# Input projections of the even block: TensorE's instructions tied to the order in which they are written

## The chip, the cores and the metric

One core of one Trainium2 chip runs the whole program. The metric is the device time of one execution in microseconds (us), as the median of several runs.

## The reference, cut to what matters

The model is a chain of blocks on 1024 tokens of width 1024. The change touches the first one, the even block, and in it only the products of the normed tokens `h` and the normed context `hc` with the input weights. The filters of the next block (`hyena_filters` and their Fourier transforms) and the modulation vectors of blocks 0 and 1 do not depend on `h`; the kernel computes them beside these products.

```python
shift, scale, gate = modulation(c[:, None, :], w_mod[i], b_mod[i])
h = rmsnorm(x, norm_g[i]) * (1 + scale) + shift
hc = rmsnorm(ctx, norm_g[i]) * (1 + cscale) + cshift
a_val, a_gate, q, k, v, b_gate = jnp.split(h @ w_in, EVEN_SPLITS, axis=-1)
q = apply_rope(rmsnorm(to_heads(q, N_Q_HEADS), q_norm_g[li]), cos, sin)
k = apply_rope(rmsnorm(to_heads(k, N_KV_HEADS), k_norm_g[li]), cos, sin)
ck, cv = jnp.split(hc @ w_in[:, EVEN_SPLITS[2]:EVEN_SPLITS[4]], 2, axis=-1)
...
def modulation(cond, w_mod, b_mod):
    m = jax.nn.silu(cond) @ w_mod + b_mod
```

## The kernel before, in words

**The products.** Every float32 product of an activation and a weight is made of three matmuls on rounded halves (`mm3`, L200 to L204): high by high, low by high, high by low. `gemm` (L206) does that for the eight slices of the inner dimension, 24 matmuls of 512 columns for one half of the tokens. `ev_in` (L440) makes 18 panels of 128 output columns for all 1024 tokens with it, 48 matmuls a panel: six gates (PSUM tile `pbg`), two pool values and two pool gates (`pav`, `pag`), six queries (`pq`) and two keys (`pk`, with the context's keys `pck` ahead of each), and then the values (`pv`). The first two gates are done together, half by half (`pg2`), so that their first 96 matmuls can start on the half of the tokens that is normed first. A panel's PSUM tile has two buffers, small PSUM tiles share four buffers (`psb`).

**The side work.** After each slice of a `gemm`, that is after every three matmuls (six for the values), `self.go()` (L124) advances three generators, each at its own rate:

- `K.hy`, rate 0.7: `hy_prep` (L856), which makes the filters' spectra in 12 units (`hy_spectrum`, L888). A unit has four tap products `pf` (L902, L903), column sums `pl` (L924) of the sum `hacc` that VectorE and ScalarE make of the taps, a turned row (L935), and two blocks of Fourier products `pk` (L953, L954), which VectorE then combines (`dft8`, L811). Between these steps stand bare `yield`s, among them five ahead of `pl`. The step before the first unit (`load(0)`, L864) loads the table `w`, splits it into `w3h` and `w3l` on ScalarE and VectorE, and copies each from partitions 0 to 63 to partitions 64 to 127 by a DMA from the POOL queue (L870). The taps read all 128 partitions.
- `K.ctx`, rate 0.2: the context's norm (`ctx_norm`, L367).
- `K.side`, rate 0.1: `modulation1` (L964), four times `mod_cols` (L309): eight steps, each with a DMA of 512 KB (`wm`, L315) and a multiply-add on VectorE into `macc` (L318, L320), and with the eighth step, at once, eight one-column matmuls that sum `macc` over partitions (`pm`, L220) and an addition on VectorE (L325).

```python
    def go(self):                       # class Work
        self.due += self.rate
        while self.due >= 1.0:
            self.due -= 1.0
            next(self.gen, None)
```

So the written order is fixed by counting: the n-th call of `go` runs a step of `K.hy` whenever 0.7 n passes a whole number, one of `K.side` at every tenth call. The second call runs `load(0)`, the third the first taps; the eighth steps of `mod_cols` fall on calls 80, 160, 240 and 320 of 344.

**The order on the engines.** The written order is not the order in which an engine gets its instructions. When the program is built, each engine's list is laid out anew: among the instructions whose inputs and buffers are expected to be ready by then, the one written first. On the chip each engine then takes its list in that order. What a DMA queue, VectorE, ScalarE and TensorE get is settled in this way for the whole program.

**Buffers.** Tiles of 4 KB a partition (the tables, `wm`, `hk`, `fS`, queries and so on) share 40 slots (`t`, L153). The tile of a load is given out where the load is written, and its DMA waits until the slot's last reader is done.

Of the kernel before, what the change touches and what calls it, by code (L numbers as in the profile page):

```python
# [44 lines left out]
class Work:  # L45


    def __init__(self, gen, rate=0.0):
        self.gen, self.rate, self.due = gen, rate, 0.0

    def go(self):
# [4 lines that stand above are left out]
# [48 lines left out]
class Core:  # L104
    def __init__(self, tc, ctx, d):
        self.tc, self.nc, self.d = tc, tc.nc, d
        nc = self.nc
        self.pool = ctx.enter_context(tc.tile_pool(name="sb", bufs=1))
        self.psum = ctx.enter_context(tc.tile_pool(name="ps", bufs=1, space=PSUM))
        self.dram = ctx.enter_context(tc.tile_pool(name="dr", bufs=1, space=DRAM))  # L110
        self.ident = self.c("ident", [P, P])
        make_identity(nc, self.ident)
        self.inv = self.c("inv", [P, 4])
        nc.gpsimd.memset(self.inv[:, 0:1], 1.0 / D)
        nc.gpsimd.memset(self.inv[:, 1:2], 1.0 / P)
        nc.gpsimd.memset(self.inv[:, 2:3], 1.0)
        nc.gpsimd.memset(self.inv[:, 3:4], 0.0)
        self.mhalf = self.c("mhalf", [P, 8])
        nc.gpsimd.memset(self.mhalf, -0.5)
        self.vec = self.c("vec", [P, NVEC])  # L120
        nc.sync.dma_start(self.vec, d["vecs"])
        self.work = []

    def go(self):  # L124
        for w in self.work:
            w.go()

    def steps(self, n):
        for _ in range(n):
            self.go()  # L130
# [2068 lines left out]
def build(tc, d, out):  # L2199
    with ExitStack() as ctx:  # L2200
        K = Core(tc, ctx, d)
        K.hy = Work(K.hy_prep(), 0.7)
        hs, hc = K.ev_norm()
        K.load_consts()
        K.ctx = Work(K.ctx_norm(hc), 0.2)
        K.side = Work(K.modulation1(), 0.1)
        K.work = [K.hy, K.ctx, K.side]
        ks, vs, scls = K.ev_in(hs, hc)
        K.hy.drain()
        K.side.drain()  # L2210
        K.side = Work(K.s5_prep(), 0.25)
        K.work = [K.side]
        y = K.ev_attn(ks, vs, scls)
        x1_d = K.scr("x1_d", [KT, P, L])
        K.side.rate = 0.14
        hs = K.ev_out(y, x1_d)
        K.side.rate = 0.02
        y = K.od_mix(hs)
        K.side.rate = 0.1
        K.od_out(y, x1_d)  # L2220
        K.work = []
        K.block2(out)
# [14 lines left out]
```

## Time and profile before

| | us |
|---|---|
| median of 3 runs (4068.89 to 4072.51) | 4070.12 |
| the profiled execution | 4067.31 |
| its span | 4065.5 |
| TensorE busy in the span | 3800.5 |
| mean granted TensorE clock, share of full | 0.967 |

The span runs from the first to the last instruction of the program. The page gives busy time by engine, forty slices of the span, the DMA queues, the chain that ended last, and the costliest groups of instructions. The input projections lie between 57 and 534 us of the span: the first `pbg` matmul starts at 57.4, the last `pv` matmul ends at 534.1. The stage is read below by windows, by the waits of TensorE, and by the timeline. A busy window's clock is the share of full speed that was granted: 1.00 is 2.4 GHz, 0.50 is 1.2 GHz.

### The profile page before, as it was taken

Reading aid. Unit: us, or ns where it says so; the run is one execution under the profiler, and the core shown is the slowest. Engines: PE = TensorE matmul, PEld = TensorE weight load, DVE = VectorE, ACT = ScalarE, POOL = GpSimd, SP = SyncE. Lnnn points to the kernel's source line nnn. Section 1 sums busy time; section 2 is a strip of 40 time slices with the busy share of each in tenths; the row PEclk is TensorE's granted clock in tenths of the full one; section 3 lists DMA queues with packets and bytes.
Section 4 is the critical chain, followed back from the end, with each engine's and each line's share of the span. In section 5 each row is a group of like instructions: output and inputs, shape, how many; then the busy total and the mean of one; then the engine's idle time right before and its main releaser. Section 6 shows DMA issues by size and latency. Waiting matters only on the chain.

```text
span 4065.5 us, 51267 instructions
## 1 busy us (share of the span) xinstructions
PE 3800.5 (93%) x19684; PEld 3145.8 (77%) x19684; DVE 2841.9 (70%) x4892; ACT 1445.5 (36%) x2328; POOL 308.7 (8%) x533
## 2 busy tenths in 40 slices
PE   7899899899999997799999999989999899999998
PEld 4778788778788866687788888878787677888886
DVE  5676767786888778667866664458878867666545
ACT  3222245533111221433423333335555634332332
POOL 0001100041010022000000000011010000000000
PEclk8999999999999998999999999989999899999999
DMA  6433321063222248513322245323232332122443
GB/s 235 138 113 128 111 77 42 28 212 130 73 73 74 98 148 253 164 53 103 125 80 76 94 153 171 122 83 99 73 99 73 89 124 109 73 94 78 170 159 111
DMA packets 172907, 458.35 MB, mean 113 GB/s; under 512 B 38542, under 2 KB 59028, under 8 KB 172662
## 3 DMA queue, kind: packets, MB, share of 16 engines
q1 hardware_dynamic: 129254, 317.94, 23.8%
q0 software_dynamic: 41104, 132.41, 9.9%
q10 hardware_dynamic: 2304, 4.72, 0.3%
q8 instruction: 155, 2.54, 0.3%
q14 instruction: 90, 0.74, 0.1%
HBM read 327.07 MB, written 100.66 MB: 105 GB/s over the span
## 4 chain that ended last, share of the span: by engine, by line
PE 75%; DVE 13%; issue 4%; DMA 3%; ACT 3%; POOL 1%; SPq 0%; POOLq 0%; DVEq 0%; ACTq 0%
PE p L202 7%; PE p L203 7%; PE p L204 7%; PE pd L202 4%; PE pd L204 4%; PE pd L203 4%; PE pout L202 2%; PE pout L204 2%; PE pout L203 2%; DVE sbm L1964 2%; PE pu L202 2%; PE pu L204 2%; PE pu L203 2%; PE pwt L1985 1%; PE pz L1047 1%
## 5 line engine op out<-in xcount | busy, mean ns | idle before, releaser
L185 DVE TENSOR_TENSOR wl<-wt,wh 128x1024 fp32r<-128x1024 f32 x232 | 283.3, 1222 | 276.5 <-ACT wh L184 274.1
L184 ACT CAST wh<-wt 128x1024 fp32r<-128x1024 f32 x232 | 242.9, 1048 | 653.5 <-PE pd L203 189.9
L202 PE MATMUL p<-tq,wq 128*128 128x512 f32 x736 | 290.5, 395 | 3.6 <-ACT wq L215 3.6
L203 PE MATMUL p<-tq,wq 128*128 128x512 f32 x736 | 290.0, 394 | 0.0
L204 PE MATMUL p<-tq,wq 128*128 128x512 f32 x736 | 290.0, 394 | 0.0
L202 PE MATMUL pd<-hd,wh 128*128 128x512 f32 x704 | 277.7, 394 | 2.8 <-DVE r L1831 2.8
L204 PE MATMUL pd<-hd,wl 128*128 128x512 f32 x704 | 276.5, 393 | 0.0
L203 PE MATMUL pd<-hd,wh 128*128 128x512 f32 x704 | 276.3, 393 | 0.0
L203 PE MATMUL p<-hq,wq 128*128 128x512 f32 x480 | 189.7, 395 | 0.0
L202 PE MATMUL p<-hq,wq 128*128 128x512 f32 x480 | 189.4, 395 | 0.0
L204 PE MATMUL p<-hq,wq 128*128 128x512 f32 x480 | 189.0, 394 | 0.0
L215 ACT CAST wq<-ws 128x512 fp32r<-128x512 f32 x184 | 114.3, 622 | 208.7 <-PE p L204 204.0
L1723 DVE TENSOR_TENSOR fsg<-fsg,p 128x512 f32<-128x512 f32 x140 | 94.4, 686 | 117.1 <-PE p L204 117.1
L202 PEld LDWEIGHTS p<-tq,wq 128*128 128x128 f32 x736 | 138.1, 188 | 43.3 <-ACT wq L215 4.9
L204 PEld LDWEIGHTS p<-tq,wq 128*128 128x128 f32 x736 | 138.3, 188 | 32.2
L203 PEld LDWEIGHTS p<-tq,wq 128*128 128x128 f32 x736 | 138.2, 188 | 30.6
L1723 DVE TENSOR_TENSOR fsu<-fsu,p 128x512 f32<-128x512 f32 x140 | 94.5, 687 | 93.7 <-PE p L204 93.6
L216 DVE TENSOR_TENSOR wq<-ws,wq 128x512 fp32r<-128x512 f32 x184 | 126.7, 690 | 46.4 <-ACT wq L215 44.5
L202 PEld LDWEIGHTS pd<-hd,wh 128*128 128x128 f32 x704 | 132.2, 188 | 33.9 <-DVE r L1831 4.2
L204 PEld LDWEIGHTS pd<-hd,wl 128*128 128x128 f32 x704 | 132.2, 188 | 31.2 <-DVE wl L185 0.6
L203 PEld LDWEIGHTS pd<-hd,wh 128*128 128x128 f32 x704 | 132.2, 188 | 30.0
L202 PE MATMUL pu<-hq,wh 128*128 128x512 f32 x320 | 129.8, 406 | 9.5 <-DVE cv L984 9.5
(702 smaller groups left out, 10657.4 us busy)
## 6 DMA issues: line engine op xcount, KB each, us to landing
wt<-w_gu SPq DMA_DIRECT2D x88, 512.0 KB
wt<-w_dn SPq DMA_DIRECT2D x88, 512.0 KB
wm<-w_mod SPq DMA_DIRECT2D x48, 512.0 KB
hid<-fsg POOLq DMA_DIRECT2D x44, 512.0 KB, 3.9
hr<-hid SPq DMA_DIRECT2D x44, 512.0 KB
wt<-w_od SPq DMA_DIRECT2D x28, 512.0 KB
khat<-fX POOLq DMA_DIRECT2D x24, 512.0 KB, 3.0
kh<-khat SPq DMA_DIRECT2D x24, 512.0 KB
```

The lines of the kernel that those rows point to most:

```text
L184: nc.scalar.copy(wh, wt)
L185: nc.vector.tensor_tensor(wl, wt, wh.bitcast(F32), op=ALU.subtract)
L202: mm(ps, lh, rh, start=first, stop=False)
L203: mm(ps, lh, rl, start=False, stop=False)
L204: mm(ps, ll, rh, start=False, stop=last)
L215: self.nc.scalar.copy(h, src)
L216: self.nc.vector.tensor_tensor(l, src, h.bitcast(F32), op=ALU.subtract)
L1047: mm(p4[:, i, q], tb[:, m], z[:, self.POS[m]], start=True, stop=False)
L1723: add = lambda o, u, v: tt(o, u, v, op=ALU.add)
L1964: nc.vector.tensor_tensor_scan(om[:, :n - 1], om[:, :n - 1], self.inv[:, 3:4].to_broadcast([P, n - 1]), 1.0, op0=ALU.mult, op1=ALU.add)
L1985: nc.tensor.transpose(pt[:, s * P:(s + 1) * P], W[x][:, c:c + P], self.ident)
```

## The change

A helper `in_order` calls a function, goes through the instructions that were written meanwhile, and ties each one of TensorE to the TensorE instruction written before it. The tie is of order alone: no semaphore is added by it. `build` wraps the call of `ev_in` in it, so all 1932 TensorE instructions that are written there, the products' and the side work's, stand on TensorE in the order in which they are written. No instruction is added or removed, and VectorE's, ScalarE's, POOL's and SP's are not tied.

```diff
         self.work = []
+        self.last = None
...
+    def in_order(self, fg):
+
+        bb = self.nc.cur_bb.bb
+        n = len(bb.instructions)
+        out = fg()
+        for i in list(bb.instructions)[n:]:
+            if i.engine == mybir.EngineType.PE:
+                if self.last:
+                    self.tc.add_manual_dep(i, self.last.name, mybir.DependencyInfo(
+                        mybir.DependencyClass.NoSync, mybir.DependencyReason.DATA), reason="in_order")
+                self.last = i
+        return out
...
-        ks, vs, scls = K.ev_in(hs, hc)
+        ks, vs, scls = K.in_order(lambda: K.ev_in(hs, hc))
```

## Rows read from the trace of the kernel before

**Rows 1.** The page: busy time by engine, and the chain that ended last

```profile
PE 3800.5 (93%) x19684; PEld 3145.8 (77%) x19684; DVE 2841.9 (70%) x4892; ACT 1445.5 (36%) x2328; POOL 308.7 (8%) x533
...
PE 75%; DVE 13%; issue 4%; DMA 3%; ACT 3%; POOL 1%; SPq 0%; POOLq 0%; DVEq 0%; ACTq 0%
```

**Rows 2.** Windows over the input projections: stretch, length, busy us by engine, PEclk, DMA

```profile
57.00:534.10 477.10, 437.98 (x2532) 370.52 (x2532) 320.00 (x601) 119.11 (x171) 47.58 (x62) 0.93 0.38 127
...
57.00:106.40 49.40, 42.02 (x213) 35.42 (x213) 35.72 (x59) 19.97 (x31) 2.55 (x3) 0.85 0.52 175
106.40:133.30 26.90, 24.05 (x138) 20.36 (x137) 18.31 (x39) 5.87 (x10) 2.88 (x5) 0.94 0.32 123
133.30:166.90 33.60, 31.26 (x177) 26.55 (x176) 21.18 (x44) 7.23 (x12) 1.65 (x3) 0.95 0.35 110
166.90:209.40 42.50, 36.06 (x189) 30.50 (x188) 23.35 (x46) 10.17 (x15) 3.20 (x6) 0.88 0.48 155
...
239.80:271.30 31.50, 31.50 (x179) 26.42 (x179) 21.70 (x42) 6.75 (x11) 1.60 (x3) 1.00 0.30 101
271.30:308.50 37.20, 31.48 (x155) 24.98 (x154) 25.12 (x50) 7.25 (x9) 1.60 (x3) 0.86 0.35 128
...
343.50:364.30 20.80, 20.80 (x121) 16.54 (x120) 12.27 (x21) 3.17 (x4) 2.80 (x3) 0.84 0.39 116
...
400.30:442.80 42.50, 39.22 (x238) 33.80 (x237) 27.73 (x52) 10.72 (x15) 4.98 (x7) 0.96 0.40 138
442.80:472.80 30.00, 25.50 (x150) 21.68 (x149) 21.58 (x41) 7.53 (x11) 3.86 (x5) 0.89 0.40 138
472.80:534.10 61.30, 56.86 (x437) 51.65 (x436) 42.31 (x81) 12.22 (x19) 7.95 (x8) 0.94 0.25 87
```

**Rows 3.** Waits of TensorE from 57 to 535 us: line, releaser, us, times, longest

```profile
PE pl L924 <- DVE hacc L918: 16.6, 6, 4.7
```

**Rows 4.** Windows, the products `pbg` alone: stretch, length, TensorE busy us (count)

```profile
57.00:82.70 25.70, 24.68 (x96) 18.91 (x96) 0.00 (x0) 0.92 0.50 170
```

**Rows 5.** Tile `w3h`, 50 to 110 us: its copy's start, and its DMA's time to landing

```profile
L870 POOL DMA_DIRECT2D w3h<-w3h x1: 579/579/579, 79.7 to 79.7; - x1
...
DMA to landing us min/median/max: 2.9/2.9/2.9
```

**Rows 6.** Timeline of TensorE: start, us, instruction, idle time before it and releaser

```profile
84.27 0.36 PE L903 MATMUL pf<-w3l,hs 128*128 128x256 f32 x1 [0.86 <-DMA w3l<-w3l]
...
90.63 1.20 PE L924 MATMUL pl<-inv,hacc 128*128 128x1 f32 x5 [4.72 <-DVE hacc L918]
...
166.54 0.39 PE L954 MATMUL pk<-hk,fsin 128*128 128x128 f32 x2
...
167.22 0.40 PE L204 MATMUL pbg<-hh,wl 128*128 128x512 f32 x1
167.46 0.39 PE L202 MATMUL pbg<-hh,wh 128*128 128x512 f32 x1
...
270.26 0.39 PE L954 MATMUL pk<-hk,fsin 128*128 128x128 f32 x2
...
399.95 0.39 PE L954 MATMUL pk<-hk,fsin 128*128 128x128 f32 x2
```

**Rows 7.** Timeline of VectorE: the eighth multiply-add of three modulation vectors

```profile
174.19 1.28 DVE L320 SCALAR_TENSOR_TENSOR macc<-wm,silu_c,macc 128x1024 f32<-128x1024 f32 x1
...
278.05 1.29 DVE L320 SCALAR_TENSOR_TENSOR macc<-wm,silu_c,macc 128x1024 f32<-128x1024 f32 x1
...
406.95 1.28 DVE L320 SCALAR_TENSOR_TENSOR macc<-wm,silu_c,macc 128x1024 f32<-128x1024 f32 x1
```

**Rows 8.** Windows around two waits: length, busy by engine, PEclk

```profile
90.60:99.00 8.40, 7.25 (x33) 6.73 (x34) 3.79 (x10) 1.03 (x3) 0.00 (x0) 0.51 0.56 226
...
118.00:122.60 4.60, 4.23 (x16) 3.59 (x17) 2.35 (x8) 0.00 (x0) 0.00 (x0) 0.64 0.00 0
```

**Rows 9.** Waits of the SP queue from 57 to 535 us

```profile
SPq L315 <- PE pk L954: 50.5, 6, 12.7
```

## The prediction, made before the changed kernel was run

> **What bounds the kernel now.** I read the page first: TensorE is busy for 93% of the span and makes 75% of the chain that ended last [rows 1], so a microsecond that TensorE loses in a stage reaches the end, and one that it saves does too, as long as the next engine is not late. Then the windows over the input projections. From 57.0 to 534.1 us TensorE is busy for 437.98 of 477.10 us [rows 2]: 39.1 us idle. Its clock is 0.93 of full on the mean, so at most another 0.07 of 477, 33 us, lies in slow clock (the two overlap, since the clock is also low while it waits). VectorE, the next engine, has 320.0 us of work there, so no other engine bounds the stage. The stretches differ: 239.8 to 271.3 us has no idle time and a clock of 1.00, while 166.9 to 209.4 loses 6.4 us idle at 0.88 and 271.3 to 308.5 loses 5.7 at 0.86 [rows 2]. Last the waits: 16.6 us of the idle time are column sums `pl` waiting for `hacc`, six times, 4.7 us at the longest [rows 3].
>
> What the change can act on is order alone. By the code's count the written order has the first taps `pf` behind nine `pbg` matmuls; the trace has all 96 `pbg` matmuls of the first two gates ahead of them, done by 82.7 us [rows 4]. So the order does change where a piece of side work was expected late: there the products were pulled ahead of it. Where the side work was in time, as in 133.3 to 166.9 and 239.8 to 271.3, the trace already follows the written order (taps, 30 product matmuls, `pl`, 9, row, `pk`), and nothing moves.
>
> **The change part by part.** The work is the same; terms are waits and slow clock, in us, plus is slower. A product matmul takes 0.24 at full clock, 167.22 to 167.46 [rows 6] (0.232 over longer runs; I use 0.232).
>
> *The first taps.* They read `w3h` and `w3l` in all partitions. `w3h`'s copy is issued at 79.7 and takes 2.9 to land [rows 5], 82.6; `w3l` lets the taps go on at 84.27 [rows 6]. What leads to these copies (the table's load, the cast behind the norm's on ScalarE, the POOL queue) hangs on no product, so I leave it where it is. Tied, TensorE has nine matmuls, is through by about 61, and stands until 84.3; 87 product matmuls wait behind the taps: 87 x 0.232 = +20.2. After so long a stand it restarts at half clock: +4.1, as in 90.6 to 99.0, 8.4 us at 0.51 [rows 8]. Against that, the 87 matmuls now cover what unit 0 of the filters leaves idle today: 4.7 ahead of `pl` and, of the 7.4 idle from 57.0 to 106.4 (49.40 less 42.02 [rows 2]), another 1.8 beside the 0.9 that stays [rows 6], and the slow 4.1 that follows: -10.6. Together +13.7. Bounds: +9.6 without the slow restart, +24.3 if nothing is covered. I take the sum, since each item is a row.
>
> *Unit 1.* Today its four taps come at once, behind unit 0, and `pl` waits 2.85 (106.4 to 133.3: 26.90 less 24.05 [rows 2]), then runs 4.6 us at 0.64, 1.7 lost [rows 8]. Written, the taps lie among products: -4.5.
>
> *The modulation sums `pm`.* This is the wait that the tie adds. The eighth `wm` load is written right ahead of its multiply-add and its sum, and its slot is often given free only by `pk`: SP waits 50.5 us in six such waits [rows 9]. Written, the first sum stands 9 product matmuls behind `pk`, the second 6, the third directly behind it. Last `pk` ends: 166.93, 270.65, 400.34, start and duration added [rows 6]. `macc` ends: 175.47, 279.34, 408.23 [rows 7]. So TensorE would wait 6.4 (175.47 less 166.93 + 9 x 0.232), 7.3 (279.34 less 270.65 + 6 x 0.232) and 7.9: 21.6, and restart slowly each time, 2.9 (the mean of 4.1 and 1.7): 8.7 more. Behind each wait are queued the products of the panel, and VectorE's addition and whatever follows it there. Today that time is filled with products pulled ahead, which are then missing. So the first two stretches give back what they lose now, at most 6.4 + 0.12 x 42.5 = 11.5 and 5.7 + 0.14 x 37.2 = 10.9 [rows 2]: net 6.4+2.9-11.5 = -2.2 and 7.3+2.9-10.9 = -0.7. Around the third nothing is lost today: +10.8. Bounds for the three: -22.4 if `macc` is in time everywhere, +30.3 if nothing is given back. The fourth sum is in the right place already. I take the waits as the rows stand, since what VectorE does between `pk` and `macc` is the transform of the same unit, which follows `pk` in both kernels.
>
> Here the Trainium skill has a rule that speaks against the change: TensorE: Matmul & The Clock Gate, section on HAM oscillation, says that an engine made to wait for a DMA between pieces of its inner loop comes back at the half rate each time, and advises to finish the inner loop ahead of the wait, which is what the pulled-ahead products do. Rows 8 agree for waits of 4.7 and 2.85 us. By the rule the four new waits cost the 4.1 + 8.7 = 12.8 of slow restarts that stand in my sum; without them the sum below would be -2.7, no change.
>
> *Later waits.* 343.5 to 364.3 has no idle time but a clock of 0.84: 3.3 [rows 2]; a written order that spaces the queries' small matmuls may give back -3, bounds -3.3 and +3. From 400.3 to 534.1 the keys and values lose 3.3+4.5+4.4 = 12.2 idle and 1.7+3.3+3.7 = 8.7 in clock [rows 2]. Some waits there are for PSUM buffers that VectorE frees late, which order doesn't cure: I take -8, bounds -20.9 and +5.
>
> *New waits of `pl`.* Written, `pl` has 30 product matmuls, 7.0, behind the last tap. The need ranges from 4.7 (unit 0: 85.9 to 90.63) to some 12 (unit 1, with unit 0's transform in VectorE's way). So each of 12 units waits between nothing and 4.9; the clean stretches say mostly nothing. I take +4 in all, bounds 0 and 59.
>
> No instruction is added, VectorE's, SP's and POOL's lists are laid out by the same rule, and the attention behind the stage starts when the values end: no other term.
>
> **Sum:** 13.7 - 4.5 - 2.2 - 0.7 + 10.8 - 3 - 8 + 4 = +10.1. On the profiled execution's 4067.3 (span 4065.5 and 1.8 around it) that is 4077.4; its median of runs stands 2.8 higher, so 4070.1 + 10 = 4080. What a measurement of this kernel can tell from no change is 0.2%, 8.1 us.
>
> **The rivals.** *The sums are in time, and it is faster.* Place: the three `pm`. If VectorE's list, laid out anew, has the eighth multiply-add ahead of the transform, `macc` is done before TensorE comes to the sum. It decides when `macc` ends within 2 us of the last `pk`. For it: the first sum's load is issued long before 166. Against it: the second and third loads wait for a slot of that very `pk` [rows 9]. Price: 30.3 less, 4080 - 30 = 4050. *It cancels.* If half of the `pm` waits go, or the keys give back 17 instead of 8, the sum is between -5 and +5: 4070. Also here: the order hardly changes because it is already the written one in most units; but the 96 matmuls ahead of the first taps speak against that. *VectorE's queue is late everywhere.* If `pl` waits half of its 59 bound, because taps, ropes and pool windows meet on VectorE, +26: 4106.
>
> **How the numbers follow.** The forecast, slower by 8 to 25, has 0.37; late everywhere 0.08; it cancels 0.30; faster 0.25. So slower 0.45, same 0.30, faster 0.25. The likeliest case gives 4080; its own range is 4078 to 4095. The range for 8 in 10 reaches to the middle of the faster case, 4050, and to 4106.
>
> **What would show it.** In the changed kernel's profile the stage's first idle time should be one of some 21 us, from about 61 to 82.6, released by the copies of `w3h` and `w3l`; the wait of 4.7 ahead of the first `pl` should be gone; three waits of `pm` for `macc`, 5 to 8 us each; and the last `pv` should end near 544 instead of 534.1. I am wrong if the copies land earlier than 79, if `pm` doesn't wait, or if `pl`'s waits exceed today's 16.6 us.

## The result, and the profile of the changed kernel

The changed kernel takes 4102.27 us (median of 4 runs, 4099.78 to 4104.96), the kernel before 4071.32: 1.0079 times as long, 95% interval 1.0065 to 1.0094. It is slower, by 31 us; 10 were forecast. The two profiled executions differ by 36.6 (4103.89 less 4067.31). Their spans, 4102.1 and 4065.5, differ by as much, and 35.0 of it arise in the stage: the last `pv` matmul ends at 569.1 instead of 534.1. In the changed kernel the lines stand 14 lower (L202 is now L216).

The page first: busy times are nearly what they were [rows 1].

```profile
PE 3806.2 (93%) x19684; PEld 3153.9 (77%) x19684; DVE 2842.9 (69%) x4892; ACT 1446.2 (35%) x2328; POOL 308.9 (8%) x533
...
PE 76%; DVE 13%; issue 4%; ACT 3%; DMA 3%; POOL 1%; SPq 0%; DVEq 0%; ACTq 0%; POOLq 0%
```

Windows over the stage (stretch, length, busy us of PE, PEld, DVE, ACT, POOL, PEclk, DMA share, GB/s), which answer to [rows 2]:

```profile
57.00:569.10 512.10, 442.28 (x2530) 374.83 (x2531) 321.15 (x600) 118.82 (x170) 47.08 (x62) 0.90 0.35 118
57.00:118.00 61.00, 39.20 (x191) 31.83 (x192) 35.55 (x63) 18.20 (x29) 2.78 (x4) 0.72 0.34 114
118.00:145.80 27.80, 25.26 (x156) 21.58 (x155) 18.05 (x34) 6.94 (x11) 2.66 (x5) 1.00 0.48 171
...
175.60:218.90 43.30, 36.00 (x189) 30.18 (x188) 23.62 (x46) 10.52 (x15) 3.20 (x6) 0.84 0.48 152
249.90:281.40 31.50, 31.50 (x179) 26.40 (x178) 21.68 (x42) 6.75 (x11) 1.60 (x3) 1.00 0.29 101
281.40:326.90 45.50, 36.94 (x190) 30.70 (x189) 26.88 (x52) 7.94 (x10) 1.60 (x3) 0.85 0.30 105
326.90:361.00 34.10, 26.37 (x128) 21.88 (x127) 21.45 (x38) 11.23 (x13) 7.05 (x7) 0.84 0.49 162
361.00:400.00 39.00, 35.25 (x187) 27.71 (x186) 27.50 (x48) 8.28 (x11) 6.66 (x8) 0.96 0.33 120
400.00:440.00 40.00, 30.43 (x156) 25.70 (x157) 19.71 (x39) 5.22 (x7) 3.86 (x5) 0.79 0.29 107
```

The first row says what kind of loss it is. TensorE is idle for 512.10 less 442.28 = 69.8 us, where it was idle for 39.1: 30.7 of the 35.0 are waiting. Only 4.3 (442.28 less 437.98) are slower running. The clean stretch stays clean: 249.9 to 281.4 is the 239.8 to 271.3 of before, 31.50 busy of 31.50 at clock 1.00, only 10 us later.

The waits of TensorE from 57 to 580 us (line, releaser, us, times, longest) say for what, beside [rows 3]:

```profile
PE pm L234 <- DVE macc L334: 20.2, 3, 8.4
PE pf L916 <- DMA w3h<-w3h: 13.8, 1, 13.8
PE pl L938 <- DVE hacc L932: 12.8, 3, 7.7
...
PE pr L247 <- POOL rs_r L242: 4.3, 1, 4.3
...
PE pf L917 <- DMA w3l<-w3l: 3.3, 1, 3.3
```

And the timeline of TensorE where each of them ends, beside [rows 6], then VectorE's last multiply-adds ahead of the three sums, beside [rows 7]:

```profile
82.11 0.55 PE L916 MATMUL pf<-w3h,hs 128*128 128x256 f32 x1 [13.77 <-DMA w3h<-w3h]
85.92 0.55 PE L917 MATMUL pf<-w3l,hs 128*128 128x256 f32 x1 [3.26 <-DMA w3l<-w3l]
...
100.41 0.84 PE L938 MATMUL pl<-inv,hacc 128*128 128x1 f32 x7
...
184.21 3.57 PE L234 MATMUL pm<-inv,macc 128*128 128x1 f32 x16 [4.38 <-DVE macc L334]
...
289.57 0.77 PE L234 MATMUL pm<-inv,macc 128*128 128x1 f32 x3 [7.45 <-DVE macc L334]
...
355.58 1.83 PE L938 MATMUL pl<-inv,hacc 128*128 128x1 f32 x8 [7.72 <-DVE hacc L932]
...
401.20 1.00 PE L938 MATMUL pl<-inv,hacc 128*128 128x1 f32 x5 [3.94 <-DVE hacc L932]
...
429.14 1.01 PE L234 MATMUL pm<-inv,macc 128*128 128x1 f32 x4 [8.37 <-DVE macc L334]
```

```profile
182.87 1.28 DVE L334 SCALAR_TENSOR_TENSOR macc<-wm,silu_c,macc 128x1024 f32<-128x1024 f32 x1
...
288.13 1.28 DVE L334 SCALAR_TENSOR_TENSOR macc<-wm,silu_c,macc 128x1024 f32<-128x1024 f32 x1
...
427.81 1.28 DVE L334 SCALAR_TENSOR_TENSOR macc<-wm,silu_c,macc 128x1024 f32<-128x1024 f32 x1
```

Most of this is as foretold: the stand ahead of the first taps, the 4.72 ahead of the first `pl` gone, three waits of `pm`. Two long waits were not expected: `pl` at 355.58 and at 401.20, both while the queries are projected.

**Where the lag grows.** Matmul ends alone don't show this, since the kernel before pulls products ahead. So TensorE's matmuls of the stage are added up in the order of each trace, each at its full-clock pitch (0.232 a product, and so on), and the ends are compared at equal work. This is an estimate from one profiled execution of each kernel, good to some 1.5 us. Positive is later than the kernel before; e2 to e10 are experiments below. The third sum is written in the sixth query; the row at 390.4 is read just ahead of its wait.

| kernel before at | what has just passed | changed | e2 | e5 | e6 | e9 | e10 |
|---|---|---|---|---|---|---|---|
| 154.2 | first two gates, filter units 0 and 1 | +8.9 | +8.1 | +1.1 | +0.6 | +9.9 | +0.3 |
| 193.8 | first sum | +10.5 | +3.0 | -4.0 | -7.2 | +11.7 | -4.9 |
| 256.8 | most of the pools | +10.5 | +5.7 | -4.0 | -7.4 | +10.9 | -4.6 |
| 325.8 | second sum, first query | +14.8 | +5.9 | -0.5 | -9.7 | +10.9 | -6.6 |
| 390.4 | most of the queries, units 7 and 8 | +29.7 | +20.1 | +12.8 | -11.7 | +11.2 | -8.8 |
| 420.4 | third sum | +44.7 | +25.6 | +16.7 | -11.6 | +30.4 | -8.8 |
| 524.4 | keys and values | +35.3 | +11.7 | +1.5 | -13.3 | +20.6 | -9.5 |

So the changed kernel loses 9 at the start, 6 around the first two sums, 15 in the queries, 15 at the third sum, and gets 9 back in the keys and values.

### The profile page after: what moved, and what is told of

The parts are those of the page before. It is cut to its first block, busy times and chain, and to the rows that moved or that the text cites. A ratio compares the mean times of both kernels' runs of the same rounds, so it can differ in the third digit from the quotient of the medians.

```text
span 4102.1 us, 51264 instructions
## 1 busy us (share of the span) xinstructions
PE 3806.2 (93%) x19684; PEld 3153.9 (77%) x19684; DVE 2842.9 (69%) x4892; ACT 1446.2 (35%) x2328; POOL 308.9 (8%) x533
## 3 DMA queue, kind: packets, MB, share of 16 engines
q10 hardware_dynamic: 2304, 4.72, 0.3%
## 4 chain that ended last, share of the span: by engine, by line
PE 76%; DVE 13%; issue 4%; ACT 3%; DMA 3%; POOL 1%; SPq 0%; DVEq 0%; ACTq 0%; POOLq 0%
PE p L216 7%; PE p L218 7%; PE p L217 7%; PE pd L216 4%; PE pd L218 4%; PE pd L217 4%; PE pout L216 2%; PE pout L218 2%; PE pout L217 2%; PE pu L216 2%; PE pu L217 2%; PE pu L218 2%; DVE sbm L1978 2%; PE pwt L1999 1%; PE pz L1061 1%
## 5 line engine op out<-in xcount | busy, mean ns | idle before, releaser
L216 PE MATMUL p<-tq,wq 128*128 128x512 f32 x736 | 291.5, 396 | 3.6 <-ACT wq L229 3.6
L216 PE MATMUL pd<-hd,wh 128*128 128x512 f32 x704 | 277.6, 394 | 2.8 <-DVE r L1845 2.8
L216 PE MATMUL p<-hq,wq 128*128 128x512 f32 x480 | 189.2, 394 | 0.0
L216 PEld LDWEIGHTS p<-tq,wq 128*128 128x128 f32 x736 | 138.4, 188 | 42.4 <-ACT wq L229 4.9
L216 PEld LDWEIGHTS pd<-hd,wh 128*128 128x128 f32 x704 | 132.2, 188 | 34.0 <-DVE r L1845 4.3
L216 PE MATMUL pu<-hq,wh 128*128 128x512 f32 x320 | 129.7, 405 | 9.5 <-DVE cv L998 9.5
```

Source lines behind the costliest of these rows:

```text
L216: mm(ps, lh, rh, start=first, stop=False)
```

## The experiments

Theory A was that the loss comes from places where a piece of side work is late and its matmul now holds up products that were pulled ahead before: the first taps, three sums, and column sums of two units. Its rival was that a fixed order costs something in general, so that freeing one place moves the loss to the next. Times are medians; the first four shared a kernel before of 4071.12, the next four 4070.51, the last three 4069.51. Edits are to the changed kernel except in e6.

**e1: the sums left out of the tie.** `loose` collects the `pm` matmuls, and `in_order` passes over them.

```diff
-            if i.engine == mybir.EngineType.PE:
+            if i.engine == mybir.EngineType.PE and i.name not in self.loose:
...
+        n = len(bb.instructions)
         self.colsum(pm, acc, 8, 2)
+        self.loose.update(i.name for i in list(bb.instructions)[n:])
```

> The four sums of the modulation vectors (pm) are left out of the tie; all else of the stage stays tied. Theory A (the loss is a sum of local waits, each where the written order has a piece of side work ahead of its inputs): the three waits of pm for macc, 20.2 us in the changed kernel, and the slow restarts behind them go, some 29 us gross; part comes back, since products pulled ahead are then missing, as in the kernel before. The lag of the changed kernel at equal work grew by about 1, 4 and 11 us over the three sums, so 16 us at the least: 4073 to 4087 us. Rival B (the tie makes one long chain through VectorE, whatever single wait is taken away turns up at the next tied instruction): at least 4097.

4090.48 (ratio 1.0043, 1.0028 to 1.0058): 12 of the 31 gone, between the two theories. The loose sums still waited 7.5 us in all, in two waits. What follows is only that the sums count; the next run asks it better.

**e2: everything tied, each sum one step later.** A further `yield` stands behind the eighth multiply-add, so that a sum is written ten calls, that is thirty products, behind its last multiply-add. A vector then takes nine steps instead of eight, so the edit also moves the loads of the second, third and fourth vector by 10, 20 and 30 calls, and the last vector ends behind the stage.

```diff
-            if k < KT - 1:
-                yield
+            yield
         pm = self.psb("pm1")
         self.colsum(pm, acc, 8, 2)
```

> Everything tied, but each sum pm is written one step of its generator later, ten calls of go behind its last multiply-add, so some 8 us of products and taps lie between. (The last of the four vectors is then finished behind the stage.) Theory A: the three waits of 4.4, 7.5 and 8.4 us vanish with their slow restarts, and nothing has to be pulled ahead: 4070 to 4080 us, at or below the kernel with the sums left free. Rival B: 4097 or more, the waits move to the taps and to pl behind.

4080.81 (1.002, 1.001 to 1.0029): 21 less, 0.8 above A's range. TensorE's waits of this kernel hold the 13.8 and the 12.6 still, and no `pm`:

```profile
PE pf L915 <- DMA w3h<-w3h: 13.8, 1, 13.8
PE pl L937 <- DVE hacc L931: 12.6, 4, 7.6
```

So where the sums are written, not the tie by itself, makes their waits. Ahead of the first sum nothing else is moved; for the other two the later loads go with it. The table shows where it came in: set beside the column of the changed kernel, 7 us at the first sum, 4 at the second, 9 at the third. The queries cost their 14 as before.

**e3: the tie begins behind the first two gates.**

```diff
-        for i in list(bb.instructions)[n:]:
+        for i in list(bb.instructions)[max(n, self.tie_from):]:
...
                 self.gemm(pg2[h][:, hv], w2[h], hs, hv)
+        self.tie_from = len(nc.cur_bb.bb.instructions)
```

> The tie begins behind the first two gates' 96 matmuls, so the first unit's taps may stand behind them again; from the third gate on everything is tied. Theory A: the stand of some 21 us ahead of the first taps goes; the changed kernel's lag there was 13 us when unit 0 was done and 9 when unit 2 was done: 4089 to 4094 us. Rival C (the start is caught up later in any case, since later stretches have idle time): 4100 or more.

4091.39 (1.0054, 1.0038 to 1.0071): 11 less, as A had it, though one of its four executions took 4102.12. The stand ahead of the first taps costs 11 in the end and not its 21: with it gone, `pl` waits 22.7 us in five waits again, instead of 12.8 in three.

**e4: only the products tied.** Whatever `go` writes is left loose.

```diff
     def go(self):
+        n = len(bb.instructions)
         for w in self.work:
             w.go()
+        self.loose.update(i.name for i in list(bb.instructions)[n:])
```

> Only the products and the small matmuls of ev_in itself are tied to each other; what the three generators write from within go is left free. Theory A (only side work placed ahead of its inputs costs): within 5 us of the kernel before, 4066 to 4076 us. Rival D (the order among the products themselves costs, since heads and keys are pulled ahead of each other in the kernel before): 4080 or more.

4077.01 (1.0016, 1.0007 to 1.0026), between the forecasts. It tells more than it was made for. With all the side work loose, its `pl` of unit 7 still waited 7.94 us, and the lag at equal work went from +1.3 to +10.0 just there (325.8 to 359.8 of the kernel before). Products tied among themselves and to `ev_in`'s own small matmuls are enough to make that wait.

**e5: e3 and e2 together.**

> Two of the earlier edits at once: the tie begins behind the first two gates, and each sum pm is written one step later. Theory A (local waits, each with its own price): the two gains add, 4102 less 11 less 22, 4066 to 4072 us, and the waits that stay are those of pl for hacc in units 7 and 8 of the filters, 7.7 and 3.9 us. Rival B (one chain): well short of the sum, 4076 or more.

4068.4 (0.9992, 0.9982 to 1.0001): no measurable difference from the kernel before. The two savings, 11 and 21, come to 34 together. The general rival falls here: two freed places gave back their sum, and no other place took it away.

**e6: the sums later, in the kernel before, nothing tied.** e2's edit at L321 and L322 of the kernel before.

> The kernel before, without any tie, but with each sum pm written one step later. Theory A: the sums cost the kernel before something too, since products are pulled ahead of them and are missing at the next pl: 166.9 to 209.4 and 271.3 to 308.5 us lose up to 11.5 and 10.9 us there; some of it goes: 4055 to 4067. Rival E (those losses are VectorE's, whatever TensorE's order): 4069 or more.

4057.39 (0.9968, 0.9955 to 0.9981): faster than both kernels, by 13 and by 45. The stretch with the first sum, 166.9 to 209.4 in [rows 2] with 6.4 idle at 0.88, is now this:

```profile
166.90:202.00 35.10, 33.77 (x194) 28.72 (x194) 22.03 (x45) 10.07 (x15) 3.19 (x6) 0.95 0.54 172
```

1.3 us idle at 0.95. And the waits of `pl`, 16.6 us in six [rows 3], have become

```profile
PE pl L923 <- DVE hacc L917: 7.6, 2, 4.7
```

As in e2, the later vectors' loads move too; 7.2 of the 13.3 that the table has at the end are there at the first sum already, where they do not. And e5 differs from this kernel only by the tie behind the first two gates, which therefore costs 11.

**e7: e5 with more room ahead of `pl` in units 7 and 8.** Eight and five `yield`s more there, and the generator's rate raised from 0.7 to 0.74 so that it still ends in time.

```diff
-        for _ in range(5):
+        n = 4 * g + 2 * o + ct
+        for _ in range({7: 13, 8: 10}.get(n, 5)):
             yield
...
-        K.hy = Work(K.hy_prep(), 0.7)
+        K.hy = Work(K.hy_prep(), 0.74)
```

> As the kernel with the start free and the sums later, and in units 7 and 8 of the filters 8 and 5 more steps between the last tap and pl, some 11 and 7 us of products; the filters' rate goes from 0.70 to 0.74 so that all units still end within the stage. Theory A: the waits of pl, 7.7 and 3.9 us, vanish with their slow restarts: 4050 to 4060, faster than the kernel before. Rival F (pl's chain waits for ScalarE and VectorE, which in those units wait for the queries' slots and the table's load, and not for time): pl waits as long as before, 4066 or more.

4077.23 (1.0013, 1.0004 to 1.0023), a miss: 9 slower than e5. Units 7 and 8 wait no longer, with 60 and 51 products between their last tap and `pl`, so F's reason does not hold, though the time lies in its range. But the rate shifted every other piece too, and new waits came up elsewhere:

```profile
PE pl L940 <- DVE hacc L933: 23.4, 6, 6.0
PE pbg L217 <- ACT bg L479: 6.7, 3, 4.0
PE pk L969 <- DVE hk L954: 5.1, 3, 3.0
PE pm L235 <- DVE hk L929: 4.7, 1, 4.7
```

It changed two things at once, so it gives no price for the queries alone.

**e8: everything tied, the first unit's table loaded ahead of the transforms' tables.**

```diff
-        self.dft_tables(("fcos", "fnsin", "fsin"))
...
         load(0)
+        self.dft_tables(("fcos", "fnsin", "fsin"))
```

> The changed kernel with all tied, but the first unit's table w is loaded ahead of the three transform tables (1.5 MB) in place of behind them. Theory A (the first taps wait for the copies of w3h and w3l): where w3h's copy is issued earlier than 79 us, the stand before the first taps shrinks by as much, and the end by about the same up to the 13 us that the start costs: 4089 to 4099 us. Rival G (the copies wait for ScalarE, which is behind the norm, and not for the load): 4100 or more.

4102.63 (1.0069, 1.0047 to 1.009): nothing gained. The stand is only split in two, since `w3h`'s copy comes earlier and `w3l`'s does not:

```profile
75.98 0.55 PE L916 MATMUL pf<-w3h,hs 128*128 128x256 f32 x1 [8.25 <-DMA w3h<-w3h]
84.87 0.55 PE L917 MATMUL pf<-w3l,hs 128*128 128x256 f32 x1 [8.34 <-DMA w3l<-w3l]
```

`w3l` is VectorE's, which makes it at 77.68, without a gap behind the norm's work from 67.77 on; that this list is what holds it was not tried apart. The profiled execution took 4089.05 and the three others 4102 to 4104. Of the 14.8 by which its span is shorter than the changed kernel's, 3.9 arise in the stage (the last `pv` ends at 565.2 instead of 569.1) and 10.9 behind it, where the two programs are written alike; why is open.

**e9: the six query panels left out of the tie**, all else tied as in the changed kernel. `mark["q"]` and `mark["k"]` are the places of the first instruction of the queries and of the keys.

```diff
-        for i in list(bb.instructions)[n:]:
+        ins = list(bb.instructions)
+        for i in ins[n:self.mark["q"]] + ins[self.mark["k"]:]:
```

> The changed kernel with the six query panels left out of the tie; the gates, the pool panels, the keys and the values stay tied. The tied kernel stands 10 us behind at the first query and some 41 behind when the last query ends. Theory A (two thirds of the loss arise in the queries: the waits of pl in two units, 7.7 and 3.9 us, the third sum's 8.4 us, and the slow restarts, since no product can be pulled ahead of what is late there): these waits are gone or shorter than 3 us, and the time is 4070 to 4082. Theory B (the loss is that of a fixed order in general, and only shows up there): the lag returns elsewhere, in the keys that are still tied, and the time is over 4090.

4087.16 (1.0046, 1.0032 to 1.006): 15 less, and 5 above A's range. The table shows why. Through the queries the lag is flat, +10.9 to +11.2, which is A; the 19 come behind, at the third sum, where the keys' products are still tied:

```profile
PE pf L921 <- DMA w3h<-w3h: 13.8, 1, 13.8
PE pm L236 <- DVE macc L336: 11.5, 3, 6.8
PE pl L943 <- DVE hacc L937: 6.1, 3, 3.7
```

A had counted that sum as freed with the queries, and it is loose, since it is written in the sixth of them. But its wait remained:

```profile
419.57 3.57 PE L236 MATMUL pm<-inv,macc 128*128 128x1 f32 x16 [6.77 <-DVE macc L336]
```

The queries' products were all done by then, at 412.80, and the first key's, of which the kernel before has 28 in this gap (401.35 to 407.99), are tied behind the context's keys `pck`, which start at 436.81. What is late in the queries can be read by counting the `pq` matmuls between the last tap of unit 7 and its `pl`, in the same view for three kernels. In the kernel before:

```profile
326.50:342.40 15.90, 14.97 (x65) 11.82 (x63) 1.97 (x2) 1.00 0.91 267
```

In the changed kernel:

```profile
340.90:355.60 14.70, 6.95 (x30) 5.30 (x29) 2.02 (x2) 0.82 0.86 264
```

In e9:

```profile
337.40:353.70 16.30, 15.02 (x65) 11.87 (x64) 2.03 (x2) 1.00 0.86 261
```

The time from taps to `pl` is the same, some 15 us. Free, TensorE fills it with 65 products (the columns after the length are busy time of TensorE, its weight loads and ScalarE); tied, with the 30 that are written there.

**e10: the sums later, tied only from the third gate to the last pool panel.** The edit is e2's with `ins[self.mark["g"]:self.mark["q"]]`, `mark["g"]` standing behind the first two gates.

> The kernel with the sums one step later (4057 untied, 4068 with all tied behind the first two gates), tied only from the third gate to the last pool panel: start, queries, keys and values are free. Theory A (an order tied where the side work is ready in time costs nothing; the 11 us between those two kernels arise in the queries): 4053 to 4061, within 4 of the untied one. Theory B (the tie costs something in every panel): 4063 to 4068.

4058.2 (0.9974, 0.9965 to 0.9984), equal to the untied e6, as A had it. Where the side work is in time, the tie costs nothing that these runs can tell. So the 11 between e5 and e6 belong to what is tied in e5 and free here, the queries, keys and values, and by the table to the queries: e5 and e10 are 0.6 apart at the pools and 21.6 near the end of the queries, and the stretch behind gives half of that back.

**e11: the sums later, tied only from the first key on** (`ins[self.mark["k"]:]`).

> The kernel with the sums one step later (4057 untied), tied only from the first key to the last value. Between the tied kernel and the one before, 8 to 11 us come back in the keys and values. Theory A (the written order is better there by itself): 4046 to 4053. Theory B (what comes back is only work that the free order had pulled ahead already, so that there is nothing to gain when the stage arrives on time): 4055 to 4063.

4056.93 (0.9973, 0.9964 to 0.9981), equal to e6: B. The written order is worth nothing there by itself. At equal work this kernel even fell from -11.2 at 390.4 to +6.1 at 420.4, and was back at -9.1 by 524.4. In that stretch most of a loss is given back.

## Why the prediction was right in direction, and too small

The forecast was 4080, with 4078 to 4095 for its own case and 4050 to 4106 for 8 in 10. The measured 4102.27 lies in the wide range and above the narrow one. The lag at equal work splits by the same steps as the sum did; it is read from the profiled executions, which are 36.6 apart where the medians are 31. The forecast +4 for `pl` was for all twelve units and is set beside the queries, where the long waits came:

| step of the prediction | forecast | measured |
|---|---|---|
| first taps and unit 1 (13.7 - 4.5) | +9.2 | +8.9 |
| first sum | -2.2 | +1.6 |
| second sum | -0.7 | +4.3 |
| queries: later waits -3, new waits of `pl` +4 | +1 | +14.9 |
| third sum and keys and values (10.8 - 8) | +2.8 | +5.6 |
| together | +10.1 | +35.3 |

**The first taps: right.** The forecast of some 21 us idle came as 4.34 + 13.77 + 3.26 = 21.4, in three pieces: the one not named ended with a `pr` at 66.26, which waits for the scale of the second half of the tokens from POOL. `w3h` was not earlier, the nine products were through, and the other products covered the wait of `pl` afterwards. e3 gives 11 for it.

**The waits of the sums: right in size, too small in price.** 4.38, 7.45 and 8.37 were measured, 20.2, for 6.4, 7.3 and 7.9. The reason held too: SP still waits for `pk` ahead of the `wm` loads, now 51.4 us in six waits, beside [rows 9]:

```profile
SPq L329 <- PE pk L968: 51.4, 6, 15.7
```

What was too small was the restart. It was priced at 2.9, from stretches of [rows 8] that had the clock back after 4.6 and 8.4 us. Windows of the changed kernel behind its stalls:

```profile
184.20:193.00 8.80, 8.79 (x29) 7.64 (x30) 3.98 (x6) 0.73 (x1) 1.57 (x3) 0.50 0.33 103
193.00:200.00 7.00, 7.00 (x39) 6.09 (x38) 4.74 (x9) 2.66 (x5) 0.00 (x0) 0.98 1.01 281
289.50:299.00 9.50, 9.43 (x30) 8.20 (x31) 6.74 (x18) 0.00 (x0) 0.53 (x1) 0.50 0.14 56
...
355.50:364.20 8.70, 8.62 (x29) 6.73 (x30) 1.98 (x7) 0.21 (x1) 1.66 (x1) 0.52 0.19 73
...
401.20:408.20 7.00, 7.00 (x21) 5.15 (x22) 2.37 (x7) 0.00 (x0) 0.00 (x0) 0.52 0.03 13
...
429.10:435.50 6.40, 6.36 (x23) 5.78 (x24) 3.41 (x12) 0.00 (x0) 0.53 (x1) 0.50 0.39 139
```

6.4 to 9.5 us at half clock. Counting half of the busy time there as lost, they cost 4.4, 4.7 and 3.2 behind the sums, 12.3 for 8.7. This is gross: the kernel before had slow stretches too, and over the stage slower running adds only the 4.3 of above. That makes the first two sums 1.5 and 1.8 dearer than forecast, and the first wait was 2.0 shorter; the rest of the way from -2.2 and -0.7 to +1.6 and +4.3 is what the stretches were to give back, by these numbers 7.2 and 7.9 instead of 11.5 and 10.9.

The rule that was weighed (the Trainium skill, TensorE: Matmul & The Clock Gate, HAM oscillation) is that TensorE, made to wait for a DMA between pieces of its work, comes back at the half rate. These five waits ended with VectorE and not with a DMA, and the clock behind all five, 0.50 to 0.52, is as the rule has it.

**New waits of `pl`: the step that failed.** "The need ranges from 4.7 (unit 0: 85.9 to 90.63) to some 12", the prediction said, and "the clean stretches say mostly nothing". In the trace of before, unit 7's last tap and its `pl` are these:

```profile
326.19 0.28 PE L903 MATMUL pf<-w3l,hs 128*128 128x256 f32 x1
...
342.44 1.02 PE L924 MATMUL pl<-inv,hacc 128*128 128x1 f32 x8 [0.96 <-DVE hacc L918]
```

The tap ends at 326.47, and `pl` starts at 342.44 behind a last wait of 0.96 for `hacc`: a need of 16.0. The row was there and was not read, because a wait of 0.96 looked like none; it was that short only because 65 products had been pulled into the gap. Unit 8 has 10.9 us there (374.17 to 385.10), with 48 products and no wait. Written are 30 for either. Into unit 7 falls the change of table (the third `w`, whose split is VectorE's too), ahead of unit 8's sum stands a rope, and VectorE is about as late with them as it was:

```profile
347.60 1.22 DVE L230 TENSOR_TENSOR w3l<-w,w3h 64x1024 fp32r<-64x1024 f32 x1 [2.99 <-ACT w3h L229]
```

The same wait for `w3h` was 2.93 in the kernel before. Now it shows on TensorE: 7.72 and 3.94 of wait and 4.2 and 3.4 of slow restart make 19.3, less what the freer order lost there before. Forecast were +4 for all units, without a restart, and at most 4.9 of wait in one. e9 shows it from the other side: queries free, no loss there. The -3 for 343.5 to 364.3 fell with it, with 7.7 idle and a clock of 0.84 in 326.9 to 361.0. The prediction's own sign of this error, `pl` waiting for more than 16.6 us, did not show: all waits of `pl` came to 12.8, since those of units 0, 1, 3 and 6 went. The total fell while the price rose.

**Keys and values: right number by luck.** The forecast of -8 stood on order curing waits; -9.4 came back. But e11 shows that order is worth nothing there, and that the stretch gives back most of what was lost just ahead of it. That VectorE catches up while TensorE stands is the likely cause, and was not tried apart. So the +15.0 at the third sum and the -9.4 belong together. Nor are all of the 15.0 the sum's: e2, where it does not wait, still loses 5.5 there.

**The rivals.** "The sums are in time" would have been worth 30; e2, which puts them in time, was worth 21. "It cancels" asked for half of the `pm` waits to go, which did not, or for 17 back from the keys, of which 9.4 came. "VectorE's queue is late everywhere" (+26, half of a bound of 59) was nearest in size, but wrong in kind: of twelve units three wait at `pl`, two of them long, and e10 shows that the tie costs nothing from the third gate to the last pool panel.

## What to carry to other kernels

An order fixed by hand was free here where every piece of side work was in time. Where one was late it cost up to the whole wait and the restart behind it, less what the freer order lost there and what came back later. Before tying, read for each such place from when its last input is sent off to when its result is used, not the wait that is left: a short wait may be short because the free order has filled the gap. And where a late piece is found, move it in the written order first: with the sums one step later the untied kernel gained 13 us, and none of the ties tried here added to that.

## What the runs showed of the hardware that was not expected

After a stall TensorE ran at half clock for 6.4 to 9.5 us while it was busy nearly without a gap (8.79 of 8.80 us from 184.2 to 193.0). It had stood there for 1.82 and, one us of work later, for 4.38. A wait of 8.37 at 429.14 was followed by the shortest such stretch, 6.4, and one of 3.94 at 401.20 by 7.0. The length of the stand alone does not set the price here, and the mean of two rows of before, 2.9, was too low for all five (3.2 to 4.7).
